# Attention values in a two-block transformer kernel: a one-pass product with split operands, key tiles turned in pairs, and filling work spread over all blocks

## The chip, the cores and the metric

The kernel runs on one core of a Trainium2 chip. The metric is the device time of one execution in microseconds (us). The engines are TensorE (PE; PEld is its weight load), VectorE (DVE), ScalarE (ACT), GpSimd (POOL) and SyncE (SP, which here issues most transfers). Each engine works through its own list of instructions in order, and waits on semaphores of the others.

## The reference

Two transformer blocks follow each other on 512 tokens of width 1024. The change is in the first block's attention: 16 query heads in 4 groups share 4 key and value heads of 64 numbers each. A query block of 128 tokens sees the key tiles beside it within a window of 128 tokens, and 256 context tokens.

```python
def block(i):
    ...
    logits = jnp.concatenate([s_lat, s_ctx, sink_column(sink, s_lat.shape[:-1])], axis=-1)
    p = jax.nn.softmax(logits, axis=-1)
    p_lat = p[..., :span].astype(v.dtype)
    p_ctx = p[..., span:span + L].astype(v.dtype)
    return (jnp.einsum('bhgqs,bshd->bqhgd', p_lat, vb)
            + jnp.einsum('bhgqs,bshd->bqhgd', p_ctx, v_ctx))
```

Around it stand a projection `w_in`, a short convolution gate, a gated merge, a mixture of 16 experts (which reads some 200 MB of weights), and then the whole second block.

## The kernel before, in words

All is written in float32. Large products are made of three one-pass products of float32r parts: each operand is split into a first part (`wh`, `hxh`, written by ACT) and a remainder (`wl`, `hxl`, written by DVE as the difference), and `mm3` (L297 to L299) multiplies first by first, first by remainder and remainder by first.

Attention is done in 16 blocks, one for each key/value group g and query block b. A block has 4 heads and `nk` key tiles of 128: 4 tiles where b is 0 or 3, 5 tiles where it is 1 or 2, so 72 tiles over all blocks. In the loop over blocks, the scores of one block (`new`) run beside the values of the block before it (`old`). For each of five turns i the loop issues:

- `scores(i)` for i below 4: four float32r products into one PSUM tile `s` (L845, L848; there is one such tile, so the next scores wait until DVE has read it), DVE's maximum with the mask added (L851, L854), and ACT's exponential (L855);
- a share of filling work, taken from generators in `todo`: the query projections of groups 1 to 3 and the 12 column chunks of the convolution branch, 15 generators of 16 steps each, 240 steps. A step of a column chunk is one `mm3`, three products of 512 columns. Its other engines' work (splitting the next weight, the products of the convolution, the rotary embedding) is issued between the steps;
- at i = 3, `normalize`: the sink's exponential, the sum and its reciprocal (L860 to L863), and four scalings of the probabilities `P` by DVE (L865);
- one piece of `values`: the four transposes of a key tile (PE, L876, into a PSUM tile `pT`), the copy `PT` to SBUF (ACT, L878), and, one piece later, the product with `V` in plain float32 (L884), whose two calls are issued as four instructions, two for each half of the array's columns;
- a second share of filling work.

Each of the two shares in a turn is `RATE = 1.8` steps, so 18 steps in a block, until `todo` is empty; the last blocks have none. The loop has a 17th pass for the last block's values. `bank` gives PSUM tiles from a pool of six, and everything is issued in program order, without a scheduler.

After attention come the merge and the output projection, then the experts, whose weights SP loads as buffers come free.

Of the kernel before, what the change touches and what calls it, by code (L numbers as in the profile page):

```python
# [63 lines left out]
def tile_two_blocks(ctx: ExitStack, tc: tile.TileContext, a, out):  # L64
    nc = tc.nc
    ACT, DVE, PE, POOL, SP = nc.scalar, nc.vector, nc.tensor, nc.gpsimd, nc.sync
# [7 lines left out]
    def big(name, shape, dt=F32):  # L74
        return bp.tile([128] + shape, dt, name=name, tag="B")
# [24 lines left out]
    def bank(name="pb", shape=(512,), dt=F32):  # L100
        return cur["ps"].tile([128] + list(shape), dt, name=name, tag="b")
# [174 lines left out]
    class Split:  # L276
# [42 lines left out]
        for _ in gen:  # L319
            pass  # L320

    RATE = 1.8

    class Filler:

        def __init__(self):
            self.q, self.late, self.acc = [], [], 0.0

        def add(self, gen):
            self.q.append(gen)
# [12 lines left out]
        def fill(self, n):  # L345
            while n > 0 and self.q:
                try:
                    next(self.q[0])
                    n -= 1
                    self.tick()  # L350
                except StopIteration:
                    self.q.pop(0)

        def share(self, rate):
            self.acc += rate
            n = int(self.acc)
            self.acc -= n
            self.fill(n)

# [264 lines left out]


    kT = [kv.tile([128, 2, 768], F32R, name=f"kT{g}", tag=f"kT{g}") for g in range(4)]
    V = kv.tile([128, 6, 256], F32, name="V", tag="V")

    def k_post(part):
        pk = kacc[part].rearrange("p (t c) -> p t c", t=2)  # L630
# [25 lines left out]
    kvs(vacc, wv, 3, (0, 1, 2))  # L656
    kst[2] = k_post(2)
    for part in range(3):
        ACT.activation(V[:, 2 * part:2 * part + 2, :], vacc[part], AF.Copy)
    W.load(3)  # L660

    sink8 = cp.tile([128, 16], F32, name="sink8")
# [155 lines left out]
    class Block:  # L818


        def __init__(self, g, b):
            self.g, self.b = g, b
            self.kb = kb = [t for t in (b - 1, b, b + 1) if 0 <= t < NT]
            self.nl = nl = len(kb) * 128
            self.n = n = nl + 256

            if b == NT - 1:
                self.lo, self.co, self.s0, self.mask = 256, 0, 0, C("mask")[:, 0:512]
                self.keys = [4, 5] + kb
            else:  # L830
                self.lo, self.co, self.s0 = 512 - nl, 512, 512 - nl
                self.mask = C("mask")[:, 896 - n:]
                self.keys = kb + [4, 5]
            self.P = []

        def scores(self, i):
            g, kb, nl, n, lo, co = self.g, self.kb, self.nl, self.n, self.lo, self.co
# [19 lines left out]
        def normalize(self):  # L857
            g, sm = self.g, self.sm
            e4 = sp.tile([128, 4], F32, name="e4", tag="e4")
            DVE.tensor_add(e4, sink[:, 4 * g:4 * g + 4], self.m4)  # L860
            ACT.activation(e4, e4, AF.Exp)
            DVE.tensor_add(sm, sm, e4)
            DVE.reciprocal(sm, sm)  # L863
            for i in range(4):
                DVE.tensor_scalar(self.P[i][:, :self.n], self.P[i][:, :self.n], sm[:, i:i + 1], None, op0=OP.mult)  # L865

        def values(self):
            g, b, nk = self.g, self.b, self.n // 128
            po = None
            pt = None  # L870
            for kk in range(nk + 1):
                last = pt
                if kk < nk:
                    p_ = bank("pT", (4, 128))
                    for i in range(4):
                        PE.transpose(p_[:, i, :], self.P[i][:, kk * 128:kk * 128 + 128], ident)  # L876
                    pt = sp.tile([128, 2, 2, 128], F32, name="PT", tag="PT", bufs=2)
                    ACT.activation(pt, p_.rearrange("p (i h) q -> p i h q", h=2), AF.Copy)  # L878
                yield
                if kk:  # L880
                    po = po or bank("po", (2, 128))
                    vi = self.keys[kk - 1]
                    for h in range(2):
                        PE.matmul(po[64 * h:64 * h + 64], V[:, vi, g * 64:g * 64 + 64], last[:, :, h, :],  # L884
                                  start=(kk == 1), stop=(kk == nk), tile_position=(0, 64 * h))
            ACT.activation(oT[g // 2][:, 2 * (g % 2):2 * (g % 2) + 2, b * 128:b * 128 + 128], po, AF.Copy)

    def order():
        n = 0
# [17 lines left out]
    for it in todo:  # L907
        F.add(it)
    blocks = [Block(g, b) for g in range(4) for b in range(4)] + [None]
    old = None  # L910
    for n, new in enumerate(blocks):
        vals = old.values() if old else iter(())
        if new:
            while qdone[0] < new.g:
                F.fill(1)
        for i in range(5):
            if new and i < 4:
                new.scores(i)
            F.share(RATE)
            if new and i == 3:  # L920
                new.normalize()
            next(vals, None)
            F.share(RATE)
        for _ in vals:
            pass
        old = new
    F.drain()
    F.flush()
    pa.close()
# [1064 lines left out]
```

## Time and profile before

| what | value |
|---|---|
| median of 3 runs | 1671.71 us (1670.66 to 1672.89) |
| profiled execution, its own time | 1671.03 us |
| span of its trace | 1669.3 us |
| mean granted TensorE clock | 0.998 of full speed |
| PE busy over the span | 97% |
| DVE, ACT busy over the span | 55%, 34% |

The span runs from the first to the last instruction; the execution's own time holds 1.7 us more. Busy shares are averages over all stages, and a busy PE may be a slow PE, since products are pipelined: where two products start is a better measure than how long each is shown to last.

### The profile page before, as it was taken

What the parts mean: (1) busy time and instruction counts of PE and PEld (TensorE: products, weight loads), DVE (VectorE), ACT (ScalarE), POOL (GpSimd) and SP (SyncE); (2) the same over time, 40 slices, a digit from 0 to 9 for tenths busy, and PEclk for the clock granted to TensorE, in tenths of its full rate; (3) what the DMA queues carried; (4) which work ended last, traced back from release to release, by engine and by line L of the source; (5) the groups of instructions that cost most, each with busy time, mean ns of one, the idle gap of its engine ahead of it and who ended that gap; (6) DMA issues with size and microseconds to landing.
All of it is one profiled execution on the core that took longest, in us unless ns stands there. A gap on an engine that the chain in (4) does not pass through costs nothing.

```text
span 1669.3 us, 20670 instructions
## 1 busy us (share of the span) xinstructions
PE 1620.3 (97%) x8266; PEld 1138.5 (68%) x8266; DVE 924.3 (55%) x1761; ACT 569.0 (34%) x1069; POOL 60.6 (4%) x74
## 2 busy tenths in 40 slices
PE   8999999999999999999999898999999999999998
PEld 5987787767888885333333333368898888877886
DVE  4667776565564433222232222168989999845555
ACT  5454544455333233101001000062335533354334
POOL 1100000000000000000000000010101001000000
PEclk9999999999999999999999999999999999999999
DMA  9232333111554499999999999943332323323241
GB/s 367 65 104 99 101 101 102 51 51 51 193 186 151 177 377 360 408 427 427 426 426 426 427 427 426 418 163 101 83 95 76 101 76 101 109 94 101 102 151 51
DMA packets 139412, 341.26 MB, mean 204 GB/s; under 512 B 6735, under 2 KB 91508, under 8 KB 115636
## 3 DMA queue, kind: packets, MB, share of 16 engines
q1 hardware_dynamic: 135504, 328.50, 52.4%
q0 software_dynamic: 2864, 8.67, 1.4%
q10 hardware_dynamic: 948, 2.76, 0.4%
q8 instruction: 65, 1.06, 0.3%
q14 instruction: 31, 0.25, 0.0%
HBM read 333.62 MB, written 6.29 MB: 204 GB/s over the span
## 4 chain that ended last, share of the span: by engine, by line
PE 43%; DMA 13%; DVE 2%; issue 1%; ACT 1%; POOL 0%; POOLq 0%; ACTq 0%; SPq 0%; DVEq 0%
PE pb L297 9%; PE pb L298 9%; PE pb L299 9%; DMA ew<-w_exp_up 5%; DMA ew<-w_exp_gate 5%; PE py L1365 3%; DMA ew<-w_exp_down 2%; PE pu L1365 2%; DMA xe<-x_d,ix 1%; PE pv L299 1%; PE pv L297 1%; PE pv L298 1%; PE pa__6149 L1365 1%; PE pa__6391 L1365 1%; PE pa__5907 L1365 1%
## 5 line engine op out<-in xcount | busy, mean ns | idle before, releaser
L256 DVE TENSOR_TENSOR wl<-wr,wh 128x512 fp32r<-128x512 f32 x340 | 230.4, 698 | 120.4 <-ACT wh L258 120.4
L258 ACT ACTIVATE wh<-wr 128x512 fp32r<-128x512 f32 x340 | 194.6, 620 | 111.8 <-PE pb L298 58.8
L1705 DVE SCALAR_TENSOR_TENSOR co<-cin,cols,co 128x512 f32<-128x512 f32 x240 | 190.2, 792 | 4.2
L297 PE MATMUL pb<-h2h,wh 128*128 128x512 f32 x432 | 170.7, 395 | 0.0
L299 PE MATMUL pb<-h2h,wl 128*128 128x512 f32 x432 | 168.3, 390 | 0.0
L298 PE MATMUL pb<-h2l,wh 128*128 128x512 f32 x432 | 168.3, 390 | 0.0
L297 PE MATMUL pb<-hxh,wh 128*128 128x512 f32 x320 | 130.4, 408 | 0.0
L1365 PE MATMUL pu<-ew,xe 128*64 128x512 f32 x512 | 116.1, 595 | 9.9 <-DMA ew<-w_exp_up 9.8
L298 PE MATMUL pb<-hxl,wh 128*128 128x512 f32 x320 | 125.2, 391 | 0.0
L299 PE MATMUL pb<-hxh,wl 128*128 128x512 f32 x320 | 125.1, 391 | 0.0
L1365 PE MATMUL py<-ew,hb 128*64 128x512 f32 x440 | 102.4, 596 | 3.1 <-DMA ew<-w_exp_down 3.1
L297 PEld LDWEIGHTS pb<-h2h,wh 128*128 128x128 f32 x432 | 81.1, 188 | 19.0 <-issue 2.4
L1365 PEld LDWEIGHTS pu<-ew,xe 128*64 128x64 f32 x512 | 37.8, 137 | 81.1 <-issue 62.6
L299 PEld LDWEIGHTS pb<-h2h,wl 128*128 128x128 f32 x432 | 81.1, 188 | 17.1
L298 PEld LDWEIGHTS pb<-h2l,wh 128*128 128x128 f32 x432 | 81.1, 188 | 16.8 <-issue 0.5
L1382 DVE TENSOR_TENSOR xr<-pg,xr 128x512 f32<-128x512 f32 x64 | 41.6, 686 | 69.0 <-PE pg L1381 67.8
L855 ACT ACTIVATE P<-P,m 128x512 f32<-128x512 f32 (+1 forms) x64 | 49.7, 777 | 85.8 <-DVE m L854 83.2
L1456 DVE TENSOR_TENSOR hb<-pu,hb 128x512 f32<-128x512 f32 x16 | 10.3, 685 | 122.2 <-PE pu L1365 77.1
L851 DVE CUSTOM_DVE_ANT_0 P<-s,cst,sink 128x512 f32<-128x512 f32 (+1 forms) x64 | 52.2, 815 | 46.3 <-PE s L848 46.0
L1365 PEld LDWEIGHTS py<-ew,hb 128*64 128x64 f32 x440 | 32.5, 137 | 61.8 <-issue 53.1
L299 PEld LDWEIGHTS pb<-hxh,wl 128*128 128x128 f32 x320 | 60.1, 188 | 13.6
L297 PEld LDWEIGHTS pb<-hxh,wh 128*128 128x128 f32 x320 | 60.2, 188 | 11.4 <-issue 2.3
(479 smaller groups left out, 3000.4 us busy)
## 6 DMA issues: line engine op xcount, KB each, us to landing
ew<-w_exp_gate SPq DMA_DIRECT2D x64, 1024.0 KB, 19.4
ew<-w_exp_up SPq DMA_DIRECT2D x64, 1024.0 KB, 19.5
wr<-w_in SPq DMA_DIRECT2D x58, 1024.0 KB, 5.8
ew<-w_exp_down SPq DMA_DIRECT2D x55, 1024.0 KB, 20.5
wr<-w_mod SPq DMA_DIRECT2D x16, 1024.0 KB, 5.0
wm<-w_mod SPq DMA_DIRECT2D x8, 1024.0 KB, 12.4
wr<-w_out SPq DMA_DIRECT2D x8, 1024.0 KB, 4.9
ew<-w_exp_down SPq DMA_DIRECT2D x16, 512.0 KB, 10.3
```

What stands on the lines that cost most here:

```text
L256: (lo_engine or DVE).tensor_tensor(lo[:, ks], raw[:, ks], hi[:, ks].bitcast(F32), op=OP.subtract)
L258: ACT.activation(hi[:, ks], raw[:, ks], AF.Copy)
L297: PE.matmul(ps, ah, bh, start=first, stop=False)
L298: PE.matmul(ps, ah, bl, start=False, stop=False)
L299: PE.matmul(ps, al, bh, start=False, stop=last)
L851: DVE.tensor_tensor_reduce(p_[:, :n], s2[:, self.s0:self.s0 + n], self.mask, 1.0, sink8[:, 4 * g + i:4 * g + i + 1], op0=OP.add, op1=OP.ma ...
L855: ACT.activation(p_[:, :n], p_[:, :n], AF.Exp, bias=m4[:, i:i + 1], scale=0.125, accum_out=sm[:, i:i + 1])
L1365: PE.matmul(ps[64 * e:64 * e + 64, n], lhs(k, e), tiles[e][kk][:, n * 512:n * 512 + 512], start=(k == 0), stop=(k == KT - 1), tile_positio ...
L1382: DVE.tensor_add(xrow(t, half(n)), p_, xrow(t, half(n)))
L1456: DVE.tensor_mul(hb[:, 0, n * 512:n * 512 + 512], pu[:, n], hb[:, 0, n * 512:n * 512 + 512])
L1705: DVE.scalar_tensor_tensor(co[ct], cin[ct][:, k:k + 512], ctap(k, ct), co[ct], op0=OP.mult, op1=OP.add)
```

## The change

Four things change in the attention stage.

The values' product becomes a float32r product. `V` is split once into two parts, side by side in the free dimension (`Vx`, `Vc`), so that one weight load holds first part and remainder as 128 columns. `P`, transposed, is split too: ACT writes the first part `PT0`, DVE subtracts it from the PSUM tile for the remainder `PT1` (`second`). For each key tile two products of 512 columns follow (`value`), and at the end of a block `put` adds the two halves of the result (two ACT copies of 64 partitions, two DVE additions).

The scalings of `P` move from DVE to ACT (`scale`), two at i = 3 and two at i = 4.

Key tiles are turned in pairs: at i = 0, 2 and 4 the products of the pair before and the eight transposes of a pair, at i = 1 and 3 the pair's two subtractions. The fifth tile of a five-tile block is turned at i = 4, subtracted after that turn's last share, and multiplied in the next block's turn 0 (`late`).

The filling work is shared evenly: the steps that are left, divided by the shares that are left, 240 over 170, 1.41 a share.

```diff
-        def share(self, rate):
-            self.acc += rate
-            n = int(self.acc)
+        def share(self):
+
+            self.acc += self.steps / self.shares if self.steps > 0 else 0
+            self.shares -= 1
+            n = int(self.acc + 1e-6)
...
-        ACT.activation(V[:, 2 * part:2 * part + 2, :], vacc[part], AF.Copy)
+        v8 = (Vc if part == 2 else Vx[:, 2 * part:2 * part + 2]).rearrange("p t g z d -> p (t g) z d")
+        va = vacc[part].rearrange("p (a d) -> p a d", d=64)
+        ACT.activation(v8[:, :, 0], va, AF.Copy)
+        DVE.tensor_sub(v8[:, :, 1], va, v8[:, :, 0].bitcast(F32))
...
             DVE.reciprocal(sm, sm)
+
+        def scale(self, i):
+            ACT.activation(self.P[i][:, :self.n], self.P[i][:, :self.n], AF.Copy, scale=self.sm[:, i:i + 1])
+
+        def turn(self, kk):
+
+            p_ = bank("pT", (4, 128))
             for i in range(4):
-                DVE.tensor_scalar(self.P[i][:, :self.n], self.P[i][:, :self.n], sm[:, i:i + 1], None, op0=OP.mult)
...
+                PE.transpose(p_[:, i, :], self.P[i][:, kk * 128:kk * 128 + 128], ident)
+            pt = [sp.tile([128, 4, 128], F32R, name=f"PT{z}", tag=f"PT{z}", bufs=2) for z in range(2)]
+            ACT.activation(pt[0], p_, AF.Copy)
+            self.pt[kk] = pt + [p_]
+
+        def second(self, kk):
+            h_, l_, p_ = self.pt[kk]
+            DVE.tensor_sub(l_, p_, h_.bitcast(F32))
+
+        def value(self, kk):
...
+            for z in range(2):
+                PE.matmul(self.po, v_, self.pt[kk][z], start=(kk == 0 and not z), stop=(kk == self.nk - 1 and z == 1))
+
+        def put(self):
...
+            ACT.activation(to[lo_], ph[hi_, :, 0], AF.Copy)
+            ACT.activation(to[hi_], ph[lo_, :, 1], AF.Copy)
+            DVE.tensor_add(o_[lo_], ph[lo_, :, 0], to[lo_])
+            DVE.tensor_add(o_[hi_], ph[hi_, :, 1], to[hi_])
+
+        def values(self, c):
+
+            if c % 2:
+                self.second(c - 1)
+                self.second(c)
+                return
+            if c:
+                self.value(c - 2)
+                self.value(c - 1)
+            for kk in range(c, min(c + 2, self.nk)):
+                self.turn(kk)
+            if c == self.nk:
+                self.put()
...
             if new and i < 4:
                 new.scores(i)
-            F.share(RATE)
+            F.share()
             if new and i == 3:
                 new.normalize()
-            next(vals, None)
-            F.share(RATE)
-        for _ in vals:
-            pass
-        old = new
+                new.scale(0)
+                new.scale(1)
+            if not i and older:
+                older.late()
+            if old:
+                old.values(i)
+            if new and i == 4:
+                new.scale(2)
+                new.scale(3)
+            F.share()
+            if old and i == 4 and old.nk == 5:
+                old.second(4)
+        older, old = old, new
```

How the rows move shows at two places. On DVE, before, the last maximum of a block's scores (here group 0, block 2) is followed by a weight's remainder, the sink's sum `e`, the reciprocal and the four scalings:

```order
L851 ISA P,m_1509<-s_1609,cst_233,sink_835 128x640
L851 ISA m_1509 128x1
L854 TENSOR_SCALAR m_1509<-m_1509 128x1
L814 TENSOR_TENSOR yT_839<-pb,yT_839 128x512
L256 TENSOR_TENSOR wl<-wr,wh 128x512
L860 TENSOR_TENSOR e_1628<-sink,m_1509 128x4
L862 TENSOR_TENSOR sm<-sm,e_1628 128x4
L863 RECIPROCAL sm<-sm 128x4
L865 TENSOR_SCALAR P<-P,sm 128x640 x4
```

In the changed kernel, at the same place, the scalings are gone, and the old block's third and fourth remainder (`PT` from `pT`, L884) stand behind the reciprocal; the fifth (the last row) stands behind the convolution's products `zs` and `yT`:

```order
L859 TENSOR_SCALAR m_1473<-m_1473 128x1
L256 TENSOR_TENSOR wl<-wr,wh 128x512
L865 TENSOR_TENSOR e_1602<-sink,m_1473 128x4
L867 TENSOR_TENSOR sm<-sm,e_1602 128x4
L868 RECIPROCAL sm<-sm 128x4
L884 TENSOR_TENSOR PT_1575<-pT,PT_1574 128x512
L884 TENSOR_TENSOR PT_1583<-pT,PT_1582 128x512
L811 TENSOR_TENSOR zs<-pb,zs 128x512
L812 TENSOR_SCALAR yT_843<-zs,cols_92 128x512
L814 SCALAR_TENSOR_TENSOR yT_843<-zs,cols_92,yT_843 128x512 x2
L775 TENSOR_SCALAR macc<-wr,sT 128x512
L884 TENSOR_TENSOR PT_1630<-pT,PT_1629 128x512
```

So the two remainders wait in DVE's list for the whole chain of the new block's softmax. On PE, before, one tile's product (two calls) and one tile's transposes stand between steps of filling work and the scores `s`:

```order
L299 MATMUL pb<-hxh_150,wl 128x512
L884 MATMUL po<-PT,V 64x256 x2
L876 MATMUL pT<-cst,P 128x128 x4
L297 MATMUL pb<-hxh_150,wh 128x512
L298 MATMUL pb<-hxl_152,wh 128x512
L299 MATMUL pb<-hxh_150,wl 128x512
L845 MATMUL s_1609<-kT_682,qT 128x384 x2
L848 MATMUL s_1609<-kT_682,qT 128x256 x2
```

In the changed kernel, at turn 4 of the same pass, two tiles' products (four of 512 columns; the second of each pair of rows reads the remainder, `PT_1575` and `PT_1583` of the DVE rows above) and the fifth tile's transposes stand together, and the next block's scores follow:

```order
L299 MATMUL pb<-hxh_150,wl 128x512
L893 MATMUL po<-PT_1574,Vx 128x512
L893 MATMUL po<-PT_1575,Vx 128x512
L893 MATMUL po<-PT_1582,Vc 128x512
L893 MATMUL po<-PT_1583,Vc 128x512
L877 MATMUL pT<-cst,P 128x128 x4
L297 MATMUL pb<-hxh_149,wh 128x512
L298 MATMUL pb<-hxl_151,wh 128x512
L299 MATMUL pb<-hxh_149,wl 128x512
L850 MATMUL s_1646<-kT_682,qT 128x256 x2
L853 MATMUL s_1646<-kT_682,qT 128x256 x2
```

Four steps of filling work stand between a block's last scores and the four products in nearly every block.

## Rows read from the trace of the kernel before

**Rows 1.** The page's 40 slices of the span: PE, PE's granted clock, DMA.

```profile
PE   8999999999999999999999898999999999999998
...
PEclk9999999999999999999999999999999999999999
DMA  9232333111554499999999999943332323323241
```

**Rows 2.** Stretches of attention: us, then busy time (and count) by engine, clock, DMA.

```profile
112.00:352.00 240.00, 239.42 (x1403) 185.16 (x1401) 161.83 (x386) 114.24 (x246) 0.00 (x0) 1.00 0.29 93
352.00:392.00 40.00, 35.01 (x223) 22.05 (x223) 24.33 (x69) 24.12 (x56) 0.00 (x0) 1.00 0.08 27
...
96.00:391.00 295.00, 288.78 (x1726) 220.23 (x1725) 199.19 (x489) 147.53 (x319) 0.00 (x0) 1.00 0.26 83
```

**Rows 3.** PE in order of time (start, duration), one tile's product between filling steps.

```profile
130.32 0.40 PE L299 MATMUL pb<-hxh,wl 128*128 128x512 f32 x1
130.65 0.65 PE L884 MATMUL po<-PT,V 128*64 128x256 f32 x4
131.23 0.50 PE L297 MATMUL pb<-hxh,wh 128*128 128x512 f32 x1
131.57 0.40 PE L298 MATMUL pb<-hxl,wh 128*128 128x512 f32 x1
```

**Rows 4.** PE in order of time, one tile's transposes between filling steps.

```profile
134.55 0.39 PE L299 MATMUL pb<-hxh,wl 128*128 128x512 f32 x1
134.78 0.60 PE L876 MATMUL pT<-cst,P 128*128 128x128 f32 x4
...
135.45 0.40 PE L298 MATMUL pb<-hxl,wh 128*128 128x512 f32 x1
```

**Rows 5.** PE in order of time, a block's last scores to its next filling steps.

```profile
350.55 0.40 PE L297 MATMUL pb<-hxh,wh 128*128 128x512 f32 x1
...
351.24 0.39 PE L297 MATMUL pb<-hxh,wh 128*128 128x512 f32 x1
...
351.70 0.39 PE L299 MATMUL pb<-hxh,wl 128*128 128x512 f32 x1
352.01 0.65 PE L884 MATMUL po<-PT,V 128*64 128x256 f32 x4
352.60 0.66 PE L876 MATMUL pT<-cst,P 128*128 128x128 f32 x4
...
353.34 0.39 PE L298 MATMUL pb<-hxl,wh 128*128 128x512 f32 x1
```

**Rows 6.** PE in order of time where filling work has run out.

```profile
356.98 0.60 PE L876 MATMUL pT<-cst,P 128*128 128x128 f32 x4
358.13 0.62 PE L845 MATMUL s<-kT,qT 128*128 128x384 f32 x2 [0.55 <-DVE m L851]
```

**Rows 7.** Waits of PE from 352 to 392 us: total us, times, longest.

```profile
PE s L845 <- DVE m L851: 3.0, 6, 0.6
PE po L884 <- ACT PT L878: 1.8, 4, 1.0
```

**Rows 8.** PE, then DVE, in order of time: last scores and softmax chain of group 2, block 0.

```profile
270.40 0.40 PE L297 MATMUL pb<-hxh,wh 128*128 128x512 f32 x1
...
272.75 0.18 DVE L863 RECIPROCAL sm<-sm 128x4 f32<-128x4 f32 x1
```

**Rows 9.** DVE in order of time: softmax chain of group 3, block 0.

```profile
353.11 0.69 DVE L256 TENSOR_TENSOR wl<-wr,wh 128x512 fp32r<-128x512 f32 x1 [1.40 <-ACT wh L258]
...
354.34 0.18 DVE L863 RECIPROCAL sm<-sm 128x4 f32<-128x4 f32 x1
```

**Rows 10.** Groups of instructions: count, busy us, mean ns; idle before, and releaser.

```profile
L1906 DVE TENSOR_TENSOR x4l<-pT,x4h 128x512 fp32r<-128x512 f32 x8 | 5.1, 683 | 0.1
```

**Rows 11.** DVE in order of time: two of a convolution chunk's products.

```profile
131.63 1.54 DVE L809 SCALAR_TENSOR_TENSOR yT<-zs,cols,yT 128x512 f32<-128x512 f32 x2
```

**Rows 12.** SP in order of time: the first run of expert loads.

```profile
578.66 4.72 SPq L1003 DMA_DIRECT2D ew<-w_exp_gate  x6
```

More of the change, by code (lines that the diff above doesn't have):

```diff
@@ L320, in run @@
             pass
-    RATE = 1.8
     class Filler:
         def __init__(self):
-            self.q, self.late, self.acc = [], [], 0.0
+            self.q, self.late, self.acc, self.steps = [], [], 0.0, 0
         def add(self, gen):
@@ L349, in fill @@
                     n -= 1
+                    self.steps -= 1
                     self.tick()
@@ L626, in tile_two_blocks @@
     kT = [kv.tile([128, 2, 768], F32R, name=f"kT{g}", tag=f"kT{g}") for g in range(4)]
-    V = kv.tile([128, 6, 256], F32, name="V", tag="V")
+    Vx, Vc = big("Vx", [4, 4, 2, 64], F32R), kv.tile([128, 2, 4, 2, 64], F32R, name="Vc", tag="V")
     def k_post(part):
@@ L833, in __init__ @@
                 self.keys = kb + [4, 5]
-            self.P = []
+            self.P, self.pt, self.nk = [], {}, n // 128
         def scores(self, i):
@@ L863, in normalize @@
             DVE.reciprocal(sm, sm)
+        def scale(self, i):
+            ACT.activation(self.P[i][:, :self.n], self.P[i][:, :self.n], AF.Copy, scale=self.sm[:, i:i + 1])
+        def turn(self, kk):
+            p_ = bank("pT", (4, 128))
             for i in range(4):
-                DVE.tensor_scalar(self.P[i][:, :self.n], self.P[i][:, :self.n], sm[:, i:i + 1], None, op0=OP.mult)
[L867 to L886, printed above, removed]
@@ new lines, in turn @@
+                PE.transpose(p_[:, i, :], self.P[i][:, kk * 128:kk * 128 + 128], ident)
[6 more added lines that the diff above has]
+        def value(self, kk):
+            if not kk:
+                self.po = bank("po", (4, 128))
+            vi = self.keys[kk]
+            v_ = (Vx[:, vi, self.g] if vi < 4 else Vc[:, vi - 4, self.g]).rearrange("p z d -> p (z d)")
+            for z in range(2):
+                PE.matmul(self.po, v_, self.pt[kk][z], start=(kk == 0 and not z), stop=(kk == self.nk - 1 and z == 1))
@@ new lines, in put @@
+        def put(self):
+            g, b = self.g, self.b
+            to = sp.tile([128, 2, 128], F32, name="to", tag="to", bufs=2)
+            ph = self.po.rearrange("p (i h) q -> p i h q", h=2)
+            o_ = oT[g // 2][:, 2 * (g % 2):2 * (g % 2) + 2, b * 128:b * 128 + 128]
+            lo_, hi_ = slice(0, 64), slice(64, 128)
+            ACT.activation(to[lo_], ph[hi_, :, 0], AF.Copy)
+            ACT.activation(to[hi_], ph[lo_, :, 1], AF.Copy)
+            DVE.tensor_add(o_[lo_], ph[lo_, :, 0], to[lo_])
+            DVE.tensor_add(o_[hi_], ph[hi_, :, 1], to[hi_])
@@ L888, in order, with late @@
+        def values(self, c):
[10 more added lines that the diff above has]
+                self.put()
+        def late(self):
+            if self.nk == 5:
+                self.value(4)
+                self.put()
     def order():
@@ L909, in tile_two_blocks @@
     blocks = [Block(g, b) for g in range(4) for b in range(4)] + [None]
-    old = None
+    older = old = None
+    F.steps, F.shares = 16 * len(todo), 10 * len(blocks)
     for n, new in enumerate(blocks):
-        vals = old.values() if old else iter(())
         if new:
@@ L918, in tile_two_blocks @@
                 new.scores(i)
-            F.share(RATE)
+            F.share()
             if new and i == 3:
                 new.normalize()
-            next(vals, None)
-            F.share(RATE)
-        for _ in vals:
-            pass
-        old = new
+                new.scale(0)
[11 more added lines that the diff above has]
+        older, old = old, new
+    if older:
+        older.late()
     F.drain()
```

## The prediction

> **What bounds the kernel now.** I looked first at the page's slices: PE is at 90% or more in almost all of them, at the full granted clock, and DMA is saturated only in the first slice and in the experts' [rows 1]. So a saving in attention counts if it is PE's time. The stretches say the same with a split: from 112 to 352 us PE is busy 239.4 of 240 us, while DVE has 161.8 and ACT 114.2; from 352 to 392 us PE has 35.0 of 40, though the clock is full [rows 2]. The order of time says why: filling steps end at about 355 us, and after that a scores' product waits for DVE to read the one tile `s` [rows 6]. The list of waits puts that on DVE (3.0 us) and on ACT's copy (1.8 us) [rows 7]. Attention therefore has two stages: a long one where PE is the bound, and a short one where the three engines wait on each other.
>
> The saving is handed on. The experts' loads run at the DMA limit later, but their first run starts at 578.66 us, when buffers come free behind PE's work [rows 12]; if that work ends earlier, the loads start earlier. SP's list of transfers is the same before and after, in the same order.
>
> **The values' product on PE.** Between filling products, starts are 0.23 us apart. One tile's product in plain float32 stretches 0.46 us (two gaps) to 131.57 − 130.32 = 1.25 us, so it costs 0.79 [rows 3]. In front of transposes the two together cost 353.34 − 351.70 − 0.46 = 1.18 [rows 5], and transposes alone 135.45 − 134.55 − 0.46 = 0.44 [rows 4], which leaves 0.74. The new product is two of 128x512 float32r, the form of the filling products: 0.46 a tile. Gain 0.28 to 0.33 a tile; most of the 72 stand ahead of transposes or of another value product, so I take 0.28: 20 us. The low end is by the record of the four instructions alone, 0.65 − 0.46 = 0.19 [rows 3], 13.7 us; the high end 23.8. Transposes stay 288; turning them in pairs changes no price that the rows show.
>
> The Trainium skill ("FP8 and Floating Point Precision", TensorE Precision Notes) says that true float32 takes four passes through the array. For 256 columns that would be 1024 cycles, some 0.43 us at full clock as an estimate if the two halves of the columns run side by side, and the new product's 1024 columns would take as long: by that the product would gain nothing. The trace does not agree: 0.65 us for the four records alone, 0.74 and more in the flow, against 0.46 [rows 3, 5]. What is left of this case is the fourth rival.
>
> **The last blocks.** 240 steps over 170 shares are 1.41 a share instead of 1.8, so filling work lasts to the 17th pass. What it covers again is 4.8 us by the list of waits [rows 7], 5.0 by PE's idle time [rows 2], and more by starts: 358.13 − 356.98 = 1.15 us, of which the transposes before account for 0.36 and 0.79 is late where the list shows 0.55 [rows 6]. With ten such waits at 0.24 more I get 7.2. I take 6.5.
>
> **What DVE and ACT get.** DVE loses 64 scalings and gains 72 remainders; the nearest row is the same subtraction from PSUM, 0.68 us [rows 10]. That is 49 us more, about 29 less, some 10 more for `put` (32 additions of a quarter of the elements, between 0.15 and 0.38) and 2 for `V`: about 230 of 290 us against 199 of 295 [rows 2], 80% busy. ACT gets some 45 us of scalings and goes from half to about two thirds. Neither becomes the bound by its sum. But each works in order, and PE now waits for DVE in a place where it did not.
>
> **The new wait.** At turn 4 PE multiplies tiles 2 and 3, four filling steps after the block's last scores. A step is 351.24 − 350.55 = 0.69 us [rows 5], so PE is there 2.77 us after those scores, and wants the third tile's remainder at 3.0 and the fourth's at 3.46. DVE writes both only after `normalize` of the new block, since they stand behind it in its list, and `normalize` waits for the exponential on ACT. In the trace the reciprocal ends 272.75 + 0.18 − 270.40 = 2.53 us after the scores where nothing stands between [rows 8], and 354.34 + 0.18 − 350.55 = 3.97 where ACT's and DVE's pieces of a weight do [rows 5, 9]. Two remainders add 1.37. So PE waits 3.90 − 3.46 = 0.45 us in the first case (0.65 with 640 keys, whose exponential is longer) and 1.9 in the second. By the order of the changed kernel, of the 15 blocks 7 have nothing that delays (7 × 0.55 = 4), and 8 have something: a weight's pieces, sums of the modulation, and once each the rotary embedding and a convolution's products, some 1 to 3 us. With 1.55 for these, 12.5. Sum 16.5 us.
>
> Three smaller ones. The fifth tile's remainder stands behind a convolution chunk's products in three blocks (two of these are 1.54 us [rows 11], all four about 2.7), and PE meets it in the next block's turn 0: 2.5 us. The pair at turn 2 has 3.8 us of cover and needs about 2.5; it is late twice: 1. The three remainders of `V` stand on DVE when the keys' transposes want the banks that they read: between nothing and 2 us, taken as 0.5. What is queued behind PE there is only PE's own work, so these waits add up: 20.5 us.
>
> `put`'s copies hold ACT until the product is done, but the scalings behind them are wanted by PE only after a share, the next scores and another share, 2 us later: nothing.
>
> **The sum.** 1671.0 (the profiled execution's own time, 0.7 below the median) − 20 − 6.5 + 20.5 = 1665.0 us. Most of the gain is given back, because the product no longer waits for ACT alone.
>
> **The rivals.**
> 1. *The waits are hidden.* If DVE and ACT run ahead, so that only the plain case of 0.45 to 0.65 us occurs, 15 × 0.55 = 8 and the rest nothing: 1671.0 − 26.5 + 8 = 1652.5. For it: from 112 to 352 us DVE is idle a third of the time [rows 2]. Against it: the list's order puts the weights' pieces between in about half the blocks, as in [rows 9].
> 2. *They eat all of it.* DVE at 80% has little room after a burst, so that late remainders delay the next maximum too; at 27 us of waits the time is 1671.5, no change. The rows that I have are from DVE at 67%.
> 3. *Slower.* If the reciprocal is as late as in [rows 9] in every block, each waits 1.9 us: 28.5, with the smaller ones 32.5, which gives 1677. It decides from 2.0 us a block on average, where the time passes 1675. For it: ACT takes the scalings, and is busier where the exponential must run. Against it: with 1.41 steps a share, fewer pieces fall between than with 1.8.
> 4. *The product gets no cheaper,* since the two halves already run side by side: 1685. The gaps in [rows 3] speak against it.
>
> **How the numbers follow.** The forecast (waits of 12 to 24 us, so 1656 to 1668) has 0.44; the first rival 0.15, the second 0.26, the third 0.12, the fourth 0.03. A measurement of this kernel tells changes of over 0.2%, 3.3 us, from none, so faster means below 1668.4 and slower above 1675. Faster: 0.59 (the forecast and the first); same: 0.26; slower: 0.15. The range leaves out most of the first rival and the two slower ones beyond 1676: 1655 to 1676, 8 in 10. The forecast's own is 1656 to 1668. The bounds of the product's price (13.7 and 23.8) lie within.
>
> **What would show it.** In the changed kernel's profile: the products `po` start 0.23 us apart, which would confirm the 20 us; attention's blocks are evenly long, and no scores wait for DVE after 350 us; PE's waits name `po` after DVE's `PT`, some 16 us in about 15 places at turn 4, each one just before the fourth tile's product; the first expert load lies about 6 us before 578.66. I am wrong if those waits are below 8 us or above 27 us in all, if PE's waits name the transposes after ACT's scaling instead, or if the expert stage starts earlier and ends no earlier.

## The result

| kernel | median of its runs | ratio to the kernel before, 95% interval |
|---|---|---|
| before | 1671.2 us (1670.1 to 1672.9, four runs) | 1 |
| changed | 1687.6 us (1686.2 to 1689.2, four runs) | 1.0096 [1.0084, 1.0108] |

The change makes the kernel about 16 us slower; the forecast was 1665.0 us, about 6 us faster, range 1655 to 1676. The measured time lies outside of that range.

The page's slices of the changed kernel (PE, its granted clock, DMA) look like those of before [rows 1], with one slice less of PE at its full share, in attention:

```profile
PE   8999989999999999999999898999999999999998
...
PEclk9999999999999999999999999999999999999999
DMA  9223232211455398999999999953323233333341
```

The stretches that answer to [rows 2] (us, busy time and count by engine, clock, DMA):

```profile
112.00:352.00 240.00, 220.56 (x1249) 183.92 (x1247) 178.46 (x422) 155.24 (x318) 0.00 (x0) 0.99 0.26 84
352.00:392.00 40.00, 36.74 (x185) 28.33 (x184) 27.18 (x64) 27.28 (x54) 0.00 (x0) 1.00 0.16 53
```

Where PE was busy for 239.4 of 240 us it is now for 220.6, though DVE rose only from 162 to 178 and ACT from 114 to 155. Neither is the bound by its sum. PE's waits in attention, 97 to 418 us (total us, times, longest), name what PE waited for:

```profile
PE po L893 <- DVE PT L884: 15.6, 13, 2.9
PE s L850 <- DVE m L856: 5.7, 11, 1.6
PE pb L297 <- DVE yT L819: 1.8, 1, 1.8
PE pT L877 <- ACT P L871: 1.4, 4, 0.5
PE pT L693 <- DVE PT L884: 0.9, 1, 0.9
PE pT L693 <- ACT zs L805: 0.9, 1, 0.9
```

Nearly all of the difference is there at the end of attention and is handed on. The merge's first product starts at 417.83 us instead of 401.90 (+15.9); the second block's first at 1122.76 instead of 1106.40 (+16.4); the span is 16.4 us longer. The run of six expert loads in [rows 12] moves by about the same (+15.7; two loads go ahead of it, at 434.69 us before and 450.62 after):

```profile
594.40 5.36 SPq L1050 DMA_DIRECT2D ew<-w_exp_gate  x6
```

**A measure of lateness.** The waits' list gives only time from a semaphore. I also add up, over all of PE's starts in attention, what each gap has beyond the usual one of its shapes (0.23 us between 512-column products, 0.12 at 256 columns, 0.11 between transposes; counted from 0.06 us up; the plain float32 product of before has its own prices, and so do the second product of a filling step behind transposes and the small products of the modulation). By this PE is late by 12.2 us before and by 41.1 us after. What is left of the stage is 305.9 − 12.2 = 293.7 and 320.3 − 41.1 = 279.2: PE's own work fell by 14.5 us. So −14.5 + 28.9, and 1.5 for first scores that start later (97.52 for 96.02; in the runs that have the changed kernel's code ahead of it, that start lies between 95.4 and 97.8, so this part is scatter as far as these runs tell), make the 15.9.

One of the late products, the pass with group 2's block 1 as `new` and its block 0 as `old`, in order of time (start, duration; PE's last scores, then what stands between them and the third tile's remainder):

```profile
273.99 0.62 PE L850 MATMUL s<-kT,qT 128*128 128x384 f32 x2 [0.55 <-DVE m L856]
...
275.51 1.06 ACT L879 ACTIVATE PT<-pT 128x512 fp32r<-128x512 f32 x2
...
275.64 0.69 DVE L256 TENSOR_TENSOR wl<-wr,wh 128x512 fp32r<-128x512 f32 x1 [0.91 <-ACT wh L258]
...
276.25 0.88 DVE L856 CUSTOM_DVE_ANT_0 P<-s,cst,sink 128x640 f32<-128x640 f32 x1
...
277.36 0.83 ACT L860 ACTIVATE P<-P,m 128x640 f32<-128x640 f32 x1 [0.78 <-DVE m L859]
...
277.55 0.40 PE L893 MATMUL po<-PT,Vc 128*128 128x512 f32 x1
...
278.18 0.61 ACT L258 ACTIVATE wh<-wr 128x512 fp32r<-128x512 f32 x1
...
278.83 0.69 DVE L256 TENSOR_TENSOR wl<-wr,wh 128x512 fp32r<-128x512 f32 x1 [1.51 <-ACT wh L258]
...
280.06 0.18 DVE L868 RECIPROCAL sm<-sm 128x4 f32<-128x4 f32 x1
280.16 1.25 DVE L884 TENSOR_TENSOR PT<-pT,PT 128x512 fp32r<-128x512 f32 x2
...
280.87 0.30 PEld L893 LDWEIGHTS po<-PT,Vc 128*128 128x128 f32 x2 [3.24 <-DVE PT L884]
280.87 1.10 PE L893 MATMUL po<-PT,Vc 128*128 128x512 f32 x3 [2.92 <-DVE PT L884]
```

PE multiplies the third tile's first part at 277.55 and then has nothing for 2.9 us. The remainder needs only the transposes of turn 2 and ACT's two copies, which end at 276.57; DVE reaches it at 280.16, since in its list stand a weight's remainder (which waits 0.91 us for ACT's first part), the last maximum, another weight's remainder (1.51 us of waiting for an ACT that had the exponential to do first) and the sum with its reciprocal. The Trainium skill ("TensorE: Matmul & The Clock Gate", table at the head) calls the queues of ScalarE and VectorE strictly first in, first out; the trace agrees, with those 1.51 us in which DVE stood before work that was ready.

### The profile page after: what moved, and what is told of

Read it like the earlier page. It is cut to its first block, busy times and chain, and to the rows that moved or that the text cites. A ratio compares the mean times of both kernels' runs of the same rounds, so it can differ in the third digit from the quotient of the medians.

```text
span 1685.7 us, 20501 instructions
## 1 busy us (share of the span) xinstructions
PE 1616.4 (96%) x8122; PEld 1154.5 (68%) x8122; DVE 953.8 (57%) x1804; ACT 618.2 (37%) x1149; POOL 60.5 (4%) x74
## 4 chain that ended last, share of the span: by engine, by line
PE 38%; DMA 18%; DVE 2%; issue 1%; ACT 1%; POOL 0%; POOLq 0%; SPq 0%; ACTq 0%; DVEq 0%
PE pb L297 9%; PE pb L298 9%; PE pb L299 9%; DMA ew<-w_exp_gate 6%; DMA ew<-w_exp_down 6%; DMA ew<-w_exp_up 6%; PE py L1412 2%; PE pu L1412 1%; PE pv L299 1%; PE pv L297 1%; PE pv L298 1%; PE pa__6119 L1412 1%; PE pa__6361 L1412 1%; PE py L1559 1%; PE pb L1673 1%
## 5 line engine op out<-in xcount | busy, mean ns | idle before, releaser
L297 PEld LDWEIGHTS pb<-hxh,wh 128*128 128x128 f32 x320 | 60.7, 190 | 11.4 <-DVE yT L819 2.2
L298 PEld LDWEIGHTS pb<-hxl,wh 128*128 128x128 f32 x320 | 60.8, 190 | 9.1
```

The lines of the kernel that those rows point to most:

```text
L297: PE.matmul(ps, ah, bh, start=first, stop=False)
L298: PE.matmul(ps, ah, bl, start=False, stop=False)
```

## The experiments

Each time stands with its ratio to runs of the kernel before on the same chip (their medians are 1671.3 to 1672.1 us) and that ratio's 95% interval. The changed kernel was timed only for the result above, with 1.0096 [1.0084, 1.0108]: where the interval of a run overlaps that one, as in e3, e5, e13 and e15, its difference from the changed kernel is not clear of noise. Those marked + leave out part of the computation.

**e1: even shares alone.** The kernel before, with the change's `share`.

```diff
...
-            self.acc += rate
-            n = int(self.acc)
+            self.acc += self.steps / self.shares if self.steps > 0 else 0
+            self.shares -= 1
+            n = int(self.acc + 1e-6)
...
```

> The kernel before with the filling work shared evenly and nothing else. Theory (the even share by itself covers the waits of the last blocks, which by the starts on PE are 7 to 12 us before the change): 1660 to 1664 us. Rival (fewer steps between one block's scores let waits come up in all blocks, as they did in the changed kernel with its 8 us of waits for the scores' tile): 1669 to 1676 us.

1669.7 us, 0.9988 [0.9978, 0.9998]: the rival. The last blocks' waits are gone, but block 0's scores wait 0.40 and 1.74 us, block 1's transposes 1.3, and three later scores 0.5 to 0.9, where steps had covered them. Worth 2 us, not 6.5.

**e2 +: the product alone.** The order of before, two 512-column products per tile, both with `P`'s first part (its remainder is left out), and `put`.

```diff
...
-                        PE.matmul(po[64 * h:64 * h + 64], V[:, vi, g * 64:g * 64 + 64], last[:, :, h, :], ...)
+                        PE.matmul(po, v_, last, start=(kk == 1 and not z), stop=(kk == nk and z == 1))
...
```

> The kernel before, its order and its filling kept, with the values' product changed to two float32r products of 512 columns; both read the first part of P, and the remainder of P is left out, so DVE gets no remainders. It measures the price of the product alone. If the product in the flow saves what the rows of before say (0.19 to 0.33 us a tile): 1648 to 1658 us. Rival, the product saves nothing: 1671 to 1673 us.

1671.3 us, 0.9999 [0.9989, 1.0010]: nothing, the rival. The first 13 blocks, those with filling work, are 5.4 us shorter together, but scores wait up to 2.5 us for a maximum (ahead of that one, DVE has 3.1 us of sums of the modulation and 0.9 us of `put`'s additions). In parts of the unfilled last blocks transposes start 0.21 us apart instead of 0.11 and products 0.43 instead of 0.23; the granted clock is 0.50 there (381.20 to 383.50 us, for one).

**e8 +: product and even shares.** e1 and e2 together, with `put` as two ACT copies (the product with `V`'s remainder is not added in), so that DVE gets no new work per tile or block.

```diff
...
+            ACT.activation(o_[lo_], ph[lo_, :, 0], AF.Copy)
+            ACT.activation(o_[hi_], ph[hi_, :, 1], AF.Copy)
...
```

> The kernel before with even shares and the one-pass product, both products reading the first part of P, and put reduced to two ACT copies of the product with V's first part: no work of the change is left on DVE, and the remainder of P and the sum of the two halves are left out. If the product by itself is worth 14 to 16 us on PE and only its company takes that away: 1652 to 1657 us. Rival (it is worth nothing in the flow): 1668 to 1671 us.

1654.6 us, 0.9901 [0.9883, 0.9919], as expected. PE is late by 10 us in all, 2 less than in the kernel before. So the two parts save 16.7 us together as long as DVE gets no work; even shares alone saved 2, and the product alone nothing, though that run had `put`'s additions, which this one leaves out. PE's waits:

```profile
PE s L848 <- DVE m L854: 4.9, 7, 1.6
```

**e4 +: no remainders.** The changed kernel; the second product reads the first part again.

```diff
-            DVE.tensor_sub(l_, p_, h_.bitcast(F32))
...
-                PE.matmul(self.po, v_, self.pt[kk][z], ...)
+                PE.matmul(self.po, v_, self.pt[kk][0], ...)
```

> The changed kernel without DVE's remainders; the second product reads the first part of P instead, so PE's work is the same and the remainder of P is left out of the result. Theory (remainders and their place cost about 21 us of waits at the product, 3 us of restarts behind them, and about half of the 8 us of waits for the scores): 1656 to 1664 us. Rival (the scores' waits and the uneven turns carry the loss): above 1672 us.

1665.4 us, 0.9966 [0.9953, 0.9978]. PE's lateness falls by 22 us, from 41.1 to 19.1, and the time by 22.3: the remainders, with all that they delay, cost 22 us, 1.5 times what the product saves. That is slightly above the expectation; transposes now wait 5.8 us for ACT's scalings:

```profile
PE s L850 <- DVE m L856: 6.1, 9, 1.6
PE pT L877 <- ACT P L871: 5.8, 14, 1.1
```

This run has all of the change but the remainders, e8 has only the product and the even shares: between them lie 10.8 us of time and 9 of lateness, for scalings on ACT, key tiles in pairs and `put`'s additions together.

**e11: scalings back on DVE.** The changed kernel.

```diff
-            ACT.activation(self.P[i][:, :self.n], self.P[i][:, :self.n], AF.Copy, scale=self.sm[:, i:i + 1])
+            DVE.tensor_scalar(self.P[i][:, :self.n], self.P[i][:, :self.n], self.sm[:, i:i + 1], None, op0=OP.mult)
```

> The changed kernel with the scalings of the probabilities back on DVE, at the same places (two at turn 3, two at turn 4). DVE gets some 29 us more, of which two scalings stand ahead of the third and fourth tile's remainders (0.45 us each). Theory: each of the 15 waits at turn 4 grows by about 0.8 us, 12 in all, while block 1's transposes no longer wait for ACT (2 us): 1695 to 1701. Rival (ACT, not DVE, is late at turn 4, since it holds exponential and scalings in one list): the waits fall and the time is 1678 to 1686.

1709.5 us, 1.0229 [1.0212, 1.0246]: worse than the theory's end. The waits for `PT` double, 15.6 to 30.8 us. The scalings' move to ACT is worth 22 us once there are remainders.

**e10: one tile at a time.** The changed kernel; the product of a tile stands one turn after its transposes, its remainder ahead of the next maximum.

```diff
...
-                self.value(c - 2)
                 self.value(c - 1)
...
+            if old and i < old.nk:
+                old.second(i)
...
```

> The changed kernel with key tiles turned one at a time, as before the change: at turn i the product of the tile before, then one tile's four transposes; its remainder is issued after the turn's second share, ahead of the next scores' maximum; the fifth tile as in the change. All arithmetic of the change stays. Theory (the pair's two remainders behind the chain make the wait at turn 4; with one remainder at a time only tile 3's stands there and is wanted a share later): the waits at turn 4 fall from 16 to about 5 us, the waits of the scores for DVE stay at 6 to 10 us: 1674 to 1680. Rival (72 remainders cost DVE's time wherever they stand): the waits move to the scores and the time is 1684 to 1690.

1723.1 us, 1.0305 [1.0287, 1.0323]: both theories fell, it is 35 us worse. ACT's list holds the same chain (DVE's reciprocal, ACT's scalings, ACT's copy, DVE's remainder, PE):

```profile
235.37 0.18 DVE L868 RECIPROCAL sm<-sm 128x4 f32<-128x4 f32 x1
...
235.59 1.55 ACT L871 ACTIVATE P<-P,sm 128x640 f32<-128x640 f32 x2 [0.44 <-DVE sm L868]
237.04 0.57 ACT L879 ACTIVATE PT<-pT 128x512 fp32r<-128x512 f32 x1
...
237.65 0.69 DVE L884 TENSOR_TENSOR PT<-pT,PT 128x512 fp32r<-128x512 f32 x1 [2.09 <-ACT PT L879]
...
237.67 0.50 PE L893 MATMUL po<-PT,Vc 128*128 128x512 f32 x1 [2.53 <-ACT PT L879]
```

A tile turned at turn 3 has its copy behind scalings that wait for the reciprocal. Turning in pairs avoids just that, since nothing is copied at turn 3.

**e7: 1.8 steps a share.** The changed kernel with the old rate.

```diff
-            self.acc += self.steps / self.shares if self.steps > 0 else 0
+            self.acc += 1.8
```

> The changed kernel with 1.8 filling steps a share until they run out, as before, instead of even shares. If even shares only spread the waits, the filled blocks lose about half of their waits here and the last blocks wait as long as that: 1684 to 1692 us. Rival (the thinner filling of 1.41 steps is what brings the waits up): 1672 to 1680 us.

1705.5 us, 1.0210 [1.0187, 1.0233]: both expectations fell. Even shares are worth 18 us here, 2 before. The end of the stage, without filling work, ran at this clock (us, busy times, clock):

```profile
385.00:418.00 33.00, 23.31 (x91) 18.00 (x90) 15.78 (x42) 20.16 (x42) 0.00 (x0) 0.71 0.00 1
```

**e3: remainders ahead of the chain.** The changed kernel, third and fourth remainder issued before `normalize`.

```diff
+            if old and i == 3:
+                old.values(i)
             if new and i == 3:
                 new.normalize()
...
-            if old:
+            if old and i != 3:
                 old.values(i)
```

> The changed kernel with the two remainders of turn 3 issued on DVE before the softmax's normalisation instead of behind it. Theory (the 16 us of waits at turn 4 come from that place in DVE's list): most of them go, but the normalisation ends 1.4 us later and part comes back as waits of the transposes for the scalings: 1672 to 1682 us, with PE's waits for DVE's PT down by 10 us or more. Rival (DVE is simply too busy, and any order waits as long): 1685 to 1690 us, waits for PT unchanged.

1688.1 us, 1.0098 [1.0072, 1.0123]: no gain. My theory fell; the time is the rival's, though the waits for `PT` are not unchanged. They fall from 15.6 to 11.0 us, but the reciprocal is later by two remainders, and transposes wait 5.2 us for ACT's scalings instead of 1.4. PE is late by 41.8 us in all: what stood behind the chain and the chain itself have only changed places.

**e5: weights' remainders on GpSimd.** The changed kernel in attention.

```diff
...
-                    (lo_engine or DVE).tensor_tensor(lo[:, ks], raw[:, ks], hi[:, ks].bitcast(F32), op=OP.subtract)
+                    (POOL if inatt[0] else DVE).tensor_tensor(lo[:, ks], raw[:, ks], ...)
...
```

> The changed kernel with the remainders of the weights (wl, four a chunk in attention) computed on GpSimd instead of DVE. If DVE's in-order list and its load make the waits, DVE has about 40 us less to do in attention and the pieces of a weight no longer stand in the softmax chain: the waits for PT and for the scores' tile fall by 6 to 14 us, 1674 to 1682 us. Rival (the waits are the chain from scores through the exponential to the remainder, whatever else DVE has): 1685 to 1689 us. If GpSimd is late with a weight, PE waits at a chunk's start and the time is above 1690.

1685.5 us, 1.0082 [1.0064, 1.0100]: the rival. DVE has 25 us less to do, the scores' waits fall from 5.7 to 1.0 us, those for `PT` stay (15.9). So most of the scores' waits go with DVE's work on the weights; the values' waits do not.

**e9 +: no chain.** The changed kernel without the softmax's sum, and with a constant scale.

```diff
-            DVE.tensor_add(e4, sink[:, 4 * g:4 * g + 4], self.m4)
-            ACT.activation(e4, e4, AF.Exp)
-            DVE.tensor_add(sm, sm, e4)
-            DVE.reciprocal(sm, sm)
...
-            ACT.activation(self.P[i][:, :self.n], self.P[i][:, :self.n], AF.Copy, scale=self.sm[:, i:i + 1])
+            ACT.activation(self.P[i][:, :self.n], self.P[i][:, :self.n], AF.Copy, scale=0.01)
```

> The changed kernel without the softmax chain of each block: the sink's sum, its exponential, the addition and the reciprocal are left out, and the scalings multiply by a constant (so the output is not normalized). DVE loses only three 128x4 instructions a block, some 0.5 us of its time. Theory (PE waits at turn 4 because the third and fourth tile's remainders stand in DVE's list behind a reciprocal that waits for the exponential): the 16 us of waits at turn 4 fall to 5 or less; since waits moved elsewhere in the earlier runs I take half of it as gained: 1674 to 1682. Rival (DVE is late by its load, and the chain is only what happens to stand ahead): the waits for the remainders stay above 11 us, and the time stays within 1684 to 1689.

1671.1 us, 0.9998 [0.9988, 1.0008]: 16.5 us less than the changed kernel for three short DVE instructions and a short exponential a block, more than the theory's range. ACT's scalings no longer wait for a reciprocal either. Lateness falls by 15.3 us, to 25.8. But the waits at turn 4 do not fall to 5 or less, as the theory had it: by PE's starts they go from 15.3 us to about 7.5. PE's waits:

```profile
PE po L888 <- DVE PT L879: 8.9, 8, 2.2
PE s L850 <- DVE m L856: 4.7, 7, 1.6
...
PE pT L872 <- ACT P L866: 0.4, 2, 0.2
```

What stays on `PT` at turn 4 stands behind a weight's remainder (which waits 1.51 us for ACT in the longest), the rotary embedding or the convolution's products.

**e13: `put`'s additions a turn on.** The changed kernel; the two additions stand behind the next pass's second maximum.

```diff
-            DVE.tensor_add(o_[lo_], ph[lo_, :, 0], to[lo_])
-            DVE.tensor_add(o_[hi_], ph[hi_, :, 1], to[hi_])
...
+            pend.append(adds)
...
+            if i == 1 and pend:
+                pend.pop()()
...
```

> The changed kernel with put's two DVE additions issued one turn on: put's ACT copies stay, the additions stand behind the maximum of the next pass's second scores instead of ahead of that of its first. DVE spends 15 us of the attention waiting there for ACT's copies, with that maximum queued behind. Theory (the scores' waits in the second turn, 1.6 us in four blocks, come from this, and little else does): 1683 to 1687. Rival (DVE's time in that wait is what makes the rest late, the remainders too): the waits of the values for DVE fall below 12 us and the time to 1672 to 1680.

1684.8 us, 1.0086 [1.0069, 1.0102], 2.8 less than the changed kernel, with overlapping intervals. The waits of the second scores are gone, and so is the one of 1.8 us behind the last block (`yT`, L819, which stood behind `put`'s additions); those for `PT` are not (16.6). That is as the theory had it. DVE no longer waits for ACT's copies there; the list of DVE's waits in the changed kernel (total, times, longest) had

```profile
DVE wl L256 <- ACT wh L258: 29.7, 30, 2.4
DVE P L856 <- PE s L853: 18.9, 17, 2.2
DVE oT L903 <- ACT to L902: 15.1, 12, 2.2
DVE sm L867 <- ACT e L866: 11.0, 16, 1.4
```

and now 3.6 us in the third row. Its second row grew to 28.5: most of the time came back as waiting for PE.

**e6 and e15: turn 4 later.** Products, transposes and `put` of turn 4 behind the second share; e15 also has e13's edit.

```diff
-            if old:
+            if old and i < 4:
                 old.values(i)
...
             F.share()
+            if old and i == 4:
+                old.values(i)
```

> The changed kernel with turn 4's products, transposes and put behind that turn's second share of filling work instead of ahead of it, which gives the remainders about 1 us more. Theory (each wait is what is left of a fixed delay after its cover): waits at turn 4 fall from 16 to about 7 us, 1677 to 1680 us. Rival (a wait saved there comes back at the next turn, as with the remainders first): 1685 to 1690 us.

> The changed kernel with turn 4's products, transposes and put behind the second share (as in the run that came out 10 us slower), and with put's two additions one turn on, behind the next pass's second maximum. All arithmetic of the change stays. Theory (that run lost 10 us more at the scores only because the additions, moved later with put, held the first maximum): the waits for the maximum fall from 15 to about 5 us, those for the remainders stay at 8 to 11: 1681 to 1686. Rival (the maximum is late by the remainders, or by ACT): 1693 to 1698.

e6: 1697.5 us, 1.0158 [1.0140, 1.0176]: the theory fell, 10 us worse. e15: 1684.6 us, 1.0079 [1.0062, 1.0096], as expected: the additions made all of that. It is no faster than e13 (1684.8), so the later turn 4 shows no gain of its own. PE's waits in e6, then in e15:

```profile
PE s L850 <- DVE m L856: 15.3, 16, 2.6
PE po L893 <- DVE PT L884: 8.5, 12, 2.0
```

```profile
PE po L893 <- DVE PT L884: 10.5, 14, 2.0
PE s L850 <- DVE m L856: 6.1, 7, 1.6
```

A later product makes `put` later, its additions wait for ACT, and the first maximum stands behind them.

**e16 +: both.** e9 and e13 together.

> The changed kernel without the softmax chain (sink's sum, exponential, addition and reciprocal left out, scalings by a constant) and with put's two additions one turn on. Without the chain alone it was 1671.1. Theory (both waits of DVE's list on ACT hold PE, and they add up): 1666 to 1669, with PE late by under 20 us in all. Rival (put's additions hold nothing once the chain is gone): 1670 to 1672.

1671.2 us, 0.9999 [0.9989, 1.0008]: the rival. Without the chain the additions hold nothing that PE needs; the two causes don't add up.

**e12 + and e14 +: one product per tile.** e8's order with scalings on DVE, but one product of `P`'s first part with both parts of `V`, and the change's `put`, in e14 with e13's edit. The remainder of `P` is left out; all else is computed. The edit against e8:

```diff
-                    for z in range(2):
-                        PE.matmul(po, v_, last, start=(kk == 1 and not z), stop=(kk == nk and z == 1))
+                    PE.matmul(po, v_, last, start=(kk == 1), stop=(kk == nk))
...
```

> The kernel before with even shares, scalings on DVE and one tile turned at a time, and per tile a single 512-column float32r product: the first part of the transposed probabilities with both parts of V, added by the change's put (two ACT copies, two DVE additions). It leaves out the probabilities' remainder, so that they enter rounded to float32r; nothing else is left out. By the run with two such products and no DVE work (1654.6 us) one product less for 72 tiles is 72 x 0.23 = 16.6 us: 1638 if nothing is late; with put's additions ahead of a maximum in each block, and less filling cover for each wait, 2 to 8 us more: 1640 to 1646. Rival (with less work of PE's own in a block, DVE and ACT set the pace): 1650 to 1660.

> The kernel with one float32r product per tile (the probabilities' remainder left out, as in the run before), and with put's two DVE additions one turn on, behind the next pass's second maximum. There PE lost 18.6 us to the maximum of the first scores, which stood behind additions that waited for ACT's copies. Theory (that order is the cause): the waits fall to about 5 us and the time to 1641 to 1647. Rival (the first maximum is late by DVE's or ACT's other work, and the additions only stand there): over 12 us of waits remain, 1652 to 1658.

e12: 1657.7 us, 0.9921 [0.9904, 0.9937], above the theory's range and within the rival's. e14: 1648.0 us, 0.9864 [0.9848, 0.9880], 1 us above the theory's range, with 11.4 us of waits of the scores left where the theory had 5: between theory and rival. e12's longest wait of the scores (5.3 us), ACT, then DVE, in order of time, and the sums of the scores' waits in e12 and e14:

```profile
271.23 0.38 ACT L893 ACTIVATE to<-po 64x256 f32<-64x256 f32 x1
...
271.63 0.42 DVE L894 TENSOR_TENSOR oT<-po,to 64x256 f32<-64x256 f32 x1 [2.13 <-ACT to L893]
...
272.52 0.88 DVE L854 CUSTOM_DVE_ANT_0 P<-s,cst,sink 128x640 f32<-128x640 f32 x1
```

```profile
PE s L848 <- DVE m L854: 18.6, 16, 5.3
```

```profile
PE s L848 <- DVE m L854: 11.4, 14, 2.2
```

So the order is the cause of 7 us of these waits, and of 9.7 us of time; it does not explain the other 11 us of waits. e14 beats both kernels, by 24 us the one before. Its probabilities enter the values' product rounded to float32r, as a choice of precision that the change didn't make.

## Why the prediction was wrong

**The values' product: right in kind, 5.5 us too much.** `po` starts are 0.23 us apart where nothing waits, as forecast from [rows 3]. But PE's own work fell by 14.5 us, 0.20 a tile, and not by 20. The figure is near the low end (13.7), which came from the record of the four instructions alone. So the larger one seems to have counted time around the old product that the new one did not give back in full; no run tests that.

**The wait at turn 4: right in cause and in sum, not in its exact place.** Forecast 16.5 us; measured 15.3 us by PE's starts over the 15 blocks, 16.6 with the 0.1 us by which the next start is late after each. Turn 2 cost 2.4 (forecast 1), the late fifth tile 1.8 (2.5). With the restarts 20.8 us for all three, against 20 forecast. PE stands before the third tile's remainder, not the fourth's as the prediction had it; the fourth follows with 0.1 us of delay. e9 shows the chain's part: without it turn 4's waits fall by about half, and lateness by 15 us in all. The other half stands behind pieces of weights and the convolution, which the prediction had counted too. The sizes are more uneven than forecast, from under 0.1 us in three blocks to 2.9, so that the sum came out so near is partly luck.

**The steps that failed: the last blocks, and what was put at nothing.** I took 6.5 us of waits in [rows 6, 7] as recovered, at no price, and put ACT's scalings, `put` and the turning in pairs at nothing. PE's lateness outside of the remainders is 41.1 − 20.8 = 20.3 us, against 12.2 before: 8.1 more where I had 6.5 less, 14.6 us in all.

- The even shares account for about 4.5 of these: they take steps away from other places, 1.41 instead of 1.8 there, so that e1 gained 2 us and not 6.5.
- They do not account for the rest. With even shares and product, but scalings on DVE, single tiles and no additions (e8), PE is late by 10 us, less than before the change; with all of the change but the remainders (e4), by 19.1. So what I had put at nothing costs about 9 us there.

In the changed kernel the 20.3 us stand in other places than in e4: the scores' tile, 7.8 by starts (1.76 and 0.41 in block 0 alone, as in e1); block 1's transposes behind ACT's scalings, 2.2 (in e4, 14 waits with 5.8 by the list); 1.9 behind `put`'s last additions, after the last block; and starts at the low clock, some 3. e13 puts `put`'s additions at 2.8, not clear of noise.

**The sum again.** 5.5 less gained by the product, 14.6 more lost by these steps, 0.3 from the waits of the remainders (20.8 for 20.5), and 1.5 from the stage's start: 1665.0 + 21.9 = 1686.9, where 1687.6 was measured.

**The rivals.** The first (the waits are hidden) fell: 15.3 us at turn 4 where it had 8. The third (slower, the reciprocal late in every block) has the sign right, not the cause: it wanted 1.9 us a block and the mean is 1.0. The second comes nearest in kind, "late remainders delay the next maximum too": e4 shows 22 us for the remainders with all that they delay, but they come on top of the waits of the two failed steps. The fourth fell, the product is cheaper (14.5 us, and e8). That DVE's load alone makes the remainders late is refuted by e5.

None of the prediction's three signs of being wrong came up: PE's waits for `PT` are 15.6 us, within 8 to 27, they do not name the transposes instead, and the expert stage starts later. The signs looked only at the new wait, and the terms that failed had none.

What stays open: which of scalings on ACT, pairs and `put`'s additions makes how much of the 9 us; no run takes them apart one by one without the remainders.

## What to carry to other kernels

When one engine's product needs another's result, find the place in that engine's list where the result is written, and read what stands ahead of it and what that in turn waits for: three DVE instructions of under 0.2 us and an exponential in each block cost 16 us over the stage here, while 25 us of load taken off the same engine brought 2 at most (e5, within noise). Filling work that is moved to cover one stretch uncovers another; price both, and test such parts together: even shares gave 2 us alone, the product with `put` none, and the two without `put`'s additions 17. A term that is put at nothing needs a run or a row as much as one with a price. If a wait stays when the order is turned around (e3), the chain as a whole may be too long; here, less work in it (e4, e9) helped.

## What the runs showed of the hardware

**The clock was at half after a wait inside a busy stage.** PE in order of time around a wait of 2.73 us, and the window behind it (us, busy times, clock):

```profile
239.67 0.40 PE L893 MATMUL po<-PT,Vx 128*128 128x512 f32 x1
242.80 0.79 PE L893 MATMUL po<-PT,Vx 128*128 128x512 f32 x1 [2.73 <-DVE PT L884]
243.39 1.05 PE L893 MATMUL po<-PT,Vc 128*128 128x512 f32 x2
```

```profile
243.20:244.80 1.60, 1.60 (x6) 1.20 (x6) 1.55 (x3) 0.34 (x1) 0.00 (x0) 0.50 0.00 0
```

The granted clock is 0.50 there, the lower level of 1.2 GHz, and 512-column products start 0.43 us apart. The Trainium skill ("TensorE: Matmul & The Clock Gate", Back-to-back issue gap) gives N / 1.2 ns between products of N columns at that level, by which 512 columns make an estimate of 427 ns; the trace agrees. Not every such wait is followed by it: after the longest one of the changed kernel, 2.9 us at 280.87, the next products start 0.34 us apart and then at the usual pace. And no long wait stands before the other stretch at the lower level: from 116.00 to 119.60 us the granted clock is 0.54 on average, behind four transposes of block 1 that PE started after waits of 0.3 to 0.5 us each.

**A wait costs more than itself.** In the changed kernel's attention 28 waits of PE are not followed by another wait at once. After 25 of them the next start is late as well, in 24 by about 0.1 us: 0.34 us on instead of 0.23 where both have 512 columns. The 25th is the wait before the half clock above.
